# A hybrid decoder layer on one core: convolution taps handed out per attention unit, and two gate projections laid between the heads' q, k, v

## The chip, the cores and the metric

The kernel runs on 1 core of one Trainium2 chip. The metric is the device time of one execution in microseconds (us); lower is better. A run's time is given as the median of several executions; a profile is one execution more, with its own time. Engines are named as in the profile: PE is TensorE (matrix products), DVE is VectorE, ACT is ScalarE, POOL is GpSimd, SP issues most DMAs.

## The reference

One layer works on 512 prompt tokens and on 32 sample tokens (8 sequences of 4), with 1024 channels. Three branches read the same input and are merged by sigmoid gates; a feed-forward part follows.

```python
h = x @ w_in                                    # pooling input, q, k, v, conv input, 3 x 1024 gate columns
gates = jax.nn.sigmoid(h[..., o3:] + b_gate).reshape(B, T, N_BRANCH, D_MODEL)
p, new_pool = _pool_branch(u_a, pool_buf, start_pos)
br_a = jnp.einsum('btgc,gcd->btgd', p, pool_w).reshape(B, T, D_MODEL) * pool_scale
o = stick-breaking attention of 8 heads of 64 channels
br_b = o.reshape(B, T, W_ATT) @ w_att_o
glu = c_in[..., :W_CONV] * jax.nn.sigmoid(c_in[..., W_CONV:])
cc, new_conv = _dwconv(glu, conv_buf, conv_dw, conv_b)          # causal, 31 taps, 256 channels
br_c = jax.nn.silu(_layernorm(cc, conv_ln_g, conv_ln_b)) @ conv_pw
merged = gates[:, :, 0] * br_a + gates[:, :, 1] * br_b + gates[:, :, 2] * br_c
x = layernorm(ALPHA * x + merged @ w_out);  x = layernorm(ALPHA * x + ffn(x))
```

The sample tokens also attend to 1024 older keys and values each, which lie in pages of a cache.

## The kernel before

**Layout.** Channels lie on partitions and the 544 tokens on the free axis, cut into two halves of 288 (32 sample and 256 prompt tokens) and 256. Every operand of a large product is split into a high and a low part (`split_psum`, lines 210 to 216, and `_Weights.prepare`, lines 130 to 132), and `gemm` (line 218) issues three matmuls for each of 8 blocks of 128 input channels: 24 matmuls for 128 output channels of one half, 48 for both halves, 96 for a gate group of 256 channels.

**Weights.** `_Weights` holds a list of groups in the order of their use. SP loads each group, ACT makes the high part (line 131), DVE the low part (line 132), two chunks ahead.

**Stages.** First come the pooling input, the convolution input and its gate (lines 346 to 400). Then the pooling projection (lines 495 to 510): eight rounds, each with six matmuls (line 504) into the one PSUM pair "z", which ACT (line 510) and DVE (line 508) read. `gate0(g)` (line 489) makes 256 channels of the pooling branch's gate: 96 matmuls, which ACT evicts from PSUM (line 483), a sigmoid (line 486), and two products with the merged tile `mg` on DVE (line 492). Groups 0 and 1 come ahead of attention (`NGA`), group 2 behind the first scores, group 3 in the sample stage.

**Attention.** For each pair of heads `hp`, `qkv_q`, `qkv_k` and `qkv_v` project q, k and v. Their tiles are in the pool "att", opened after the pools "s1" and "pp" of the pooling branch are closed (lines 511, 512, 604). A unit is one pair of heads and one block of 128 queries; there are 16. `front` of the next unit (scores at line 574 into "z", then DVE and ACT up to line 585) comes ahead of `back` of this one (transposes at line 595, products at line 600). Behind units 0, 1 and 2 of a pair stands one of q, k and v of the next pair.

**Convolution.** `conv_work` (line 411) is a generator of 33 steps: two for the sample tokens, then 31 with one tap of each of two channel blocks, which are DVE instructions (lines 427 and 429). `pump(n)` takes n steps. `conv_norm` (line 436) transposes the result on PE, normalizes it and writes `ch` and `cl`, which the sample stage reads. The pool "cvp" of all this is closed behind the unit loop (line 624), and then "sam" is opened, which holds the sample stage's K and V (`kr`, `vr`).

**Order.** The program is written for `tile.TileContext(nc, schedule_with_timeline_sim=True)`: the compiler orders the instructions of each engine by a list schedule, in which the order of the text gives the priority. PSUM has three banks "mm" for products by `gemm`, one pair "z", two banks "tp" and one "o".

Of the kernel before, what the change touches and what calls it, by code (L numbers as in the profile page):

```python
# [50 lines left out]
NCST = 1160  # L51
E_ID, E_RC, E_IW, E_EPS = 0, 128, 158, 160
NEARLY = 161
NGA = 2
NGB = 3
PUMP = 4
NV1 = 31
GACT = 3
VACT = False
CNU = 0  # L60
KRB = 6
LNP = (True, False)
PSM = 5
# [31 lines left out]
class _Weights:  # L95
# [39 lines left out]
    def next(self):  # L135
        i = self.at
        self.at += 1
        for j in range(i, i + 1 + self.ahead):
            self.prepare(j)
        if i + self.ahead + 1 < len(self.chunks):  # L140
            for _ in self.load(self.chunks[i + self.ahead + 1][0]):
                pass
        return self.split.pop(i)
# [3 lines left out]
def hybrid_layer_kernel(  # L147
# [37 lines left out]
    gate_group = lambda br, g: w.group(win(GO + br * D + g * 256, 256), KD, 256, ((0, 128), (128, 128)))  # L185
    w.group(pool_w.rearrange("(c s) k d -> (s k) c d", s=2), 2, 256, ((0, 256),))
    for g in range(NGA):
        gate_group(0, g)
    for hp in range(4):
        for o in (256, 768, 1280):  # L190
            w.group(win(o + hp * P, P), KD, P, ((0, 128),))
        if hp == 0:
            for g in range(NGA, NGB):
                gate_group(0, g)
    steps = []
    for g in range(4):
        steps += [(2, g), (1, g), (3, g)]
# [90 lines left out]
    def exp_set(ins):  # L288
        with tc.issue_after(ins):
            nc.scalar.preload_act_table_set("natural_log_exp_and_others")  # L290
# [35 lines left out]
    def late_constants():  # L326
        nc.sync.dma_start(ct, cst)
        nc.sync.dma_start(pix, pidx)
        nc.sync.dma_start(piv, pidv)
        nc.sync.dma_start(rwc, rowc)  # L330
        nc.sync.dma_start(sbt, sbr)
        nc.vector.scalar_tensor_tensor(out=pix, in0=pix, scalar=128.0, in1=rwc[:, 0:1].to_broadcast([P, 8 * DB]), op0=ALU.mult, op1=ALU.add)
        nc.vector.scalar_tensor_tensor(out=piv, in0=piv, scalar=32.0, in1=rwc[:, 1:2].to_broadcast([P, 2 * DB]), op0=ALU.mult, op1=ALU.add)
# [137 lines left out]
    def pump(n):  # L471
        for _ in range(n):
            next(cw, None)
# [3 lines left out]
    def gates(br, g, pool_, tag, bufs=1, **kw):  # L477
        gt = pool_.tile([P, 2, T], F32, tag=tag, bufs=bufs, name=f"gt{br}{g}", **kw)
        for m in range(2):
            for (c0, c1), ps in zip(HALVES, chunk_psums(w.next(), X, KX)):  # L480
                bias = vcol(V_BG + br * 8 + 2 * g + m)
                if br == 0 and g < GACT:
                    nc.scalar.activation(gt[:, m, c0:c1], ps[:, :c1 - c0], AF.Identity, bias=bias)
                else:
                    nc.vector.tensor_scalar(gt[:, m, c0:c1], ps[:, :c1 - c0], bias, None, op0=ALU.add)
        return gt, nc.scalar.activation(gt, gt, AF.Sigmoid)


    def gate0(g):
        gt, ins = gates(0, g, mp_, "gt", GTB)  # L490
        for m in range(2):
            nc.vector.tensor_tensor(out=mg[:, 2 * g + m], in0=mg[:, 2 * g + m], in1=gt[:, m], op=ALU.mult)
        return ins
# [19 lines left out]
    late_constants()  # L513
    for g in range(NGA):
        ins = gate0(g)


    def qkv_q(ap, hp):
        qh = ap.tile([P, NP], F32R, tag="qh", name=f"qh{hp}")
        ql = ap.tile([P, NP], F32R, tag="ql", name=f"ql{hp}")  # L520
        for hf, ps in enumerate(chunk_psums(w.next(), X, KX)):
            a = hf * PH
            split_psum(qh[:, a:a + PH], ql[:, a:a + PH], prompt_of(ps, hf), 0.125)
            for s in range(2 if hf == 0 else 0):
                r = slice(64 * s, 64 * s + 64)
                h = 2 * hp + s
                nc.scalar.mul(qbd[r, hp, :, DS * h:DS * h + DS], sview(ps[r, :NS], DS), 0.125)
        return qh, ql

    def qkv_k(ap, hp):  # L530
        kh = ap.tile([P, NP], F32R, tag="kh", name=f"kh{hp}")
        kl = ap.tile([P, NP], F32R, tag="kl", name=f"kl{hp}")
        kf = ap.tile([P, T], F32, tag="kf", bufs=1, name=f"kf{hp}")
        for hf, ps in enumerate(chunk_psums(w.next(), X, KX)):
            a = hf * PH
            split_psum(kh[:, a:a + PH], kl[:, a:a + PH], prompt_of(ps, hf))
            c0, c1 = HALVES[hf]
            nc.scalar.copy(kf[:, c0:c1], ps[:, :c1 - c0])
        nc.gpsimd.tensor_copy(ksf[:, hp], kf[:, :NS])
        nc.gpsimd.dma_start(k_t[hp * P:(hp + 1) * P], kf)  # L540
        return kh, kl
# [62 lines left out]
    with pool("att", 2, reuse_waits="tile") as ap:  # L604
        exp_set(ins.ins)
        qq, kk, vv = {0: qkv_q(ap, 0)}, {0: qkv_k(ap, 0)}, {0: qkv_v(ap, 0)}
        units = [(hp, i) for hp in range(4) for i in range(4)]
        rcs = {0: front(ap, 0, 0, qq[0], kk[0])}
        for g in range(NGA, NGB):
            ins = gate0(g)  # L610
            exp_set(ins.ins)
        for u, (hp, i) in enumerate(units):
            if u + 1 < len(units):
                h1, i1 = units[u + 1]
                rcs[u + 1] = front(ap, h1, i1, qq[h1], kk[h1])
            back(ap, hp, i, rcs.pop(u), vv[hp])
            if hp < 3 and i < 3:
                fn, d = ((qkv_q, qq), (qkv_k, kk), (qkv_v, vv))[i]
                d[hp + 1] = fn(ap, hp + 1)
            pump(PUMP)  # L620
            if u == CNU:
                pump(100)
                exp_set(conv_norm().ins)
# [88 lines left out]
    for b in range(DB):  # L712
        g = b // 2
# [7 lines left out]
        for br, g in [c for c, n_ in zip(steps, at_batch) if n_ == b]:  # L721
            if br == 2:
                gt2, ins = gates(2, g, mp_, "gt", GTB)
# [10 lines left out]
            elif br == 1:  # L734
                gt, ins = gates(1, g, g1p, f"g1{g}")
# [215 lines left out]
    def down_out(ps, r, m, hf):  # L951
        n = HALVES[hf][1] - HALVES[hf][0]
        nc.vector.tensor_tensor(out=r, in0=ps[:, :n], in1=r, op=ALU.add)

        def put(ts, n_, tp):
            nc.scalar.copy(y2[:n_, ts, m * P:(m + 1) * P], tp)

        ins = to_tokens(r, hf, put)
        if m in STAT:
            norms[hf].stats(STAT.index(m), *STATC[STAT.index(m)])  # L960
        return ins
# [23 lines left out]
    for hf in range(2):  # L985
        with tc.high_priority():
            ins = down_out(fin[hf], rr[hf], m, hf)
# [21 lines left out]
        for k, v in enumerate((v0, v1)):  # L1009
# [6 lines left out]
            for c0, c1 in ((0, D),) if hf == 0 or k == 0 else ((0, 640), (640, D)):  # L1016
                ins = nc.vector.scalar_tensor_tensor(out=v[:, c0:c1], in0=v[:, c0:c1], scalar=rs[:, k:k + 1], in1=bq[:, c0:c1], op0=ALU.mult, op1=ALU.add)
# [74 lines left out]
```

## Time and profile before

| | |
|---|---|
| median of 3 runs | 883.52 us (881.38 to 885.2) |
| the profiled execution's own time | 882.96 us |
| its span, first to last instruction | 881.2 us |
| busy: PE, DVE, ACT, POOL | 96%, 54%, 39%, 15% of the span |
| PE on the chain that ended last | 87% of the span |

A row of a busy table gives, for each engine, the time in which it had work, and in brackets the number of instructions; PEld is PE's loading of weights. PEclk is the TensorE clock that was granted, as a share of full speed. In rows of a timeline stand the start in us, the time, engine and line, operation, out<-in, and in square brackets the idle time of the engine before it and what ended it. L226 is line 226 of the kernel. Matmuls overlap in the pipeline, so that the rows' times add up to more than the stretch that they take.

### The profile page before, as it was taken

What the parts mean: (1) busy time and instruction counts of PE and PEld (TensorE: products, weight loads), DVE (VectorE), ACT (ScalarE), POOL (GpSimd) and SP (SyncE); (2) the same over time, 40 slices, a digit from 0 to 9 for tenths busy, and PEclk for the clock granted to TensorE, in tenths of its full rate; (3) what the DMA queues carried; (4) which work ended last, traced back from release to release, by engine and by line L of the source; (5) the groups of instructions that cost most, each with busy time, mean ns of one, the idle gap of its engine ahead of it and who ended that gap; (6) DMA issues with size and microseconds to landing.
All of it is one profiled execution on the core that took longest, in us unless ns stands there. A gap on an engine that the chain in (4) does not pass through costs nothing.

```text
span 881.2 us, 16355 instructions
## 1 busy us (share of the span) xinstructions
PE 847.7 (96%) x6937; PEld 801.6 (91%) x6937; DVE 476.0 (54%) x853; ACT 344.7 (39%) x575; POOL 135.4 (15%) x158
## 2 busy tenths in 40 slices
PE   7998899999999999999999999999999999999993
PEld 6997899888897678789999999999999999999993
DVE  4899956888555444468656333333333333334437
ACT  5434377777653333344414323233332233222211
POOL 1430000002457686210001000000000000000002
PEclk9999799999999999999999999999999999999997
DMA  9413222413749889663600223332233323322322
GB/s 295 122 50 101 61 86 64 143 39 93 255 135 312 285 312 331 222 234 125 193 1 1 67 78 96 97 94 65 82 96 97 96 67 90 91 83 74 104 71 102
DMA packets 96393, 110.36 MB, mean 125 GB/s; under 512 B 4416, under 2 KB 88224, under 8 KB 94144
## 3 DMA queue, kind: packets, MB, share of 16 engines
q1 hardware_dynamic: 87840, 73.12, 27.0%
q0 software_dynamic: 8480, 36.20, 11.6%
q8 instruction: 54, 0.88, 0.4%
q14 instruction: 19, 0.16, 0.1%
HBM read 104.44 MB, written 4.87 MB: 124 GB/s over the span
## 4 chain that ended last, share of the span: by engine, by line
PE 87%; DVE 7%; DMA 2%; issue 2%; POOL 1%; ACT 1%; SPq 0%; DVEq 0%; ACTq 0%; POOLq 0%
PE mm L226 77%; DVE acc L429 3%; PE z L668 2%; PE o L694 1%; PE z L574 1%; PE o L600 1%; PE tp L595 1%; DVE wl L132 1%; DMA vr<-in_cv,piv 1%; POOL kr L637 1%; PE tp L811 1%; DMA kr<-in_ck,pix 1%; DMA raw<-in_w_in 1%; PE tp L877 1%; DVE y L1015 0%
## 5 line engine op out<-in xcount | busy, mean ns | idle before, releaser
L132 DVE TENSOR_TENSOR wl<-raw,wh 128x1024 fp32r<-128x1024 f32 (+1 forms) x129 | 151.8, 1180 | 139.1 <-ACT wh L131 138.2
L131 ACT CAST wh<-raw 128x1024 fp32r<-128x1024 f32 (+1 forms) x129 | 129.3, 1006 | 237.9 <-PE mm L226 213.2
L226 PE MATMUL mm<-xh,wh 128*128 128x256 f32 (+1 forms) x672 | 199.2, 297 | 7.6 <-ACT wh L131 5.8
L226 PE MATMUL mm<-x1l,wh 128*128 128x288 f32 (+1 forms) x704 | 202.7, 288 | 0.0
L226 PE MATMUL mm<-x1h,wl 128*128 128x288 f32 (+1 forms) x704 | 201.4, 287 | 0.0
L226 PE MATMUL mm<-x1h,wh 128*128 128x288 f32 (+1 forms) x704 | 200.5, 286 | 0.1
L226 PE MATMUL mm<-xl,wh 128*128 128x256 f32 (+1 forms) x672 | 197.4, 294 | 0.2 <-DVE xl L213 0.2
L226 PE MATMUL mm<-xh,wl 128*128 128x288 f32 (+1 forms) x672 | 197.5, 295 | 0.0
L226 PEld LDWEIGHTS mm<-xh,wh 128*128 128x128 f32 x672 | 129.0, 192 | 13.0 <-ACT wh L131 6.2
L226 PEld LDWEIGHTS mm<-x1l,wh 128*128 128x128 f32 x704 | 132.2, 188 | 0.2
L226 PEld LDWEIGHTS mm<-xl,wh 128*128 128x128 f32 x672 | 128.7, 192 | 3.9 <-issue 2.9
L226 PEld LDWEIGHTS mm<-x1h,wh 128*128 128x128 f32 x704 | 132.0, 188 | 0.4 <-ACT sg L921 0.3
L226 PEld LDWEIGHTS mm<-x1h,wl 128*128 128x128 f32 x704 | 132.0, 188 | 0.0
L226 PEld LDWEIGHTS mm<-xh,wl 128*128 128x128 f32 x672 | 128.6, 192 | 3.3 <-issue 2.6
L226 PE MATMUL mm<-gl,wh 128*128 128x256 f32 (+1 forms) x352 | 101.7, 289 | 0.0
L226 PE MATMUL mm<-gh,wh 128*128 128x256 f32 (+1 forms) x352 | 101.3, 288 | 0.0
L226 PE MATMUL mm<-gh,wl 128*128 128x256 f32 (+1 forms) x352 | 100.8, 286 | 0.0
L637 POOL DMA_INDIRECT kr<-in_ck,pix x64 | 69.5, 1086 | 35.8 <-issue 14.9
L924 DVE TENSOR_TENSOR sg<-mm,sg 128x288 f32<-128x288 f32 (+1 forms) x44 | 19.4, 440 | 92.1 <-PE mm L226 92.1
L226 PEld LDWEIGHTS mm<-gl,wh 128*128 128x128 f32 x352 | 66.1, 188 | 0.1
L226 PEld LDWEIGHTS mm<-gh,wh 128*128 128x128 f32 x352 | 66.2, 188 | 0.0
L226 PEld LDWEIGHTS mm<-gh,wl 128*128 128x128 f32 x352 | 66.1, 188 | 0.0
(217 smaller groups left out, 1151.7 us busy)
## 6 DMA issues: line engine op xcount, KB each, us to landing
raw<-in_w_in SPq DMA_DIRECT2D x14, 1024.0 KB, 5.9
raw<-in_w_g SPq DMA_DIRECT2D x11, 1024.0 KB, 5.3
raw<-in_w_u SPq DMA_DIRECT2D x11, 1024.0 KB, 5.3
raw<-in_w_d SPq DMA_DIRECT2D x16, 512.0 KB, 4.1
raw<-in_w_in SPq DMA_DIRECT2D x12, 512.0 KB, 4.0
raw<-in_w_out SPq DMA_DIRECT2D x4, 1024.0 KB, 6.6
raw<-in_w_d SPq DMA_DIRECT2D x8, 384.0 KB, 3.5
raw<-in_w_att_o SPq DMA_DIRECT2D x4, 512.0 KB, 3.7
```

Source lines behind the costliest of these rows:

```text
L131: self.nc.scalar.copy(hi[:, a:b], v[:, a:b])
L132: self.nc.vector.tensor_tensor(out=lo[:, a:b], in0=v[:, a:b], in1=hi[:, a:b].bitcast(F32), op=ALU.subtract)
L226: ins = nc.tensor.matmul(ps[:, :n], lw, rr, start=first and s == 0, stop=last and s == len(steps) - 1)
L429: nc.vector.scalar_tensor_tensor(out=o, in0=v, scalar=dw, in1=o, op0=ALU.mult, op1=ALU.add)
L574: nc.tensor.matmul(zps[s][:, :wd], a[r, qs], b[r, :wd], start=n_ == 0, stop=n_ == 2)
L595: nc.tensor.transpose(tp[:, kb], rc[:, s, kb * P:(kb + 1) * P], ident)
L600: nc.tensor.matmul(op_[64 * s:64 * s + 64, :P], vtok[:, kb, 64 * s:64 * s + 64], ats[s][:, kb], start=kb == 0, stop=kb == i)
L637: nc.gpsimd.indirect_dma_start(out=kr[:, u].rearrange("p h c -> p (h c)"), out_offset=None, in_=ck, in_offset=bass.IndirectOffsetOnAxis(ap ...
L668: nc.tensor.matmul(zp[32 * jj:32 * jj + 32, :256], qbd[:, hp, b], kvt[b, "k", jj][:, :, hp], start=hp == 0, stop=hp == 3)
L694: nc.tensor.matmul(op_[32 * c:32 * c + 32], at[:, j], kvt[b, "v", j // 4][:, j % 4], start=j >= 4, stop=False)
L811: ins = nc.tensor.transpose(tp[:n, k * P:(k + 1) * P], src[:, t0 - c0:t0 - c0 + n], ident)
L924: nc.vector.tensor_tensor(out=sg, in0=pu[:, :n], in1=sg, op=ALU.mult)
```

## The change

The first gate group alone stays ahead of attention (`NGA` is 1). Groups 1 and 2 come behind unit 3 and unit 7, which are the last units of the first and of the second pair of heads, and their weights are put in that order into the list. The convolution's steps are taken three behind each unit instead of all behind unit 0, and `conv_norm` stands behind unit 12 instead of unit 0. No instruction of the layer's arithmetic is added or left out.

```diff
-NGA = 2
+NGA = 1
 NGB = 3
-PUMP = 4
+PUMP = 3
...
-CNU = 0
+CNU = 12
...
     for hp in range(4):
         for o in (256, 768, 1280):
             w.group(win(o + hp * P, P), KD, P, ((0, 128),))
-        if hp == 0:
-            for g in range(NGA, NGB):
-                gate_group(0, g)
+        if 0 < hp < 1 + NGB - NGA:
+            gate_group(0, NGA + hp - 1)
...
         rcs = {0: front(ap, 0, 0, qq[0], kk[0])}
-        for g in range(NGA, NGB):
-            ins = gate0(g)
-            exp_set(ins.ins)
         for u, (hp, i) in enumerate(units):
...
             if hp < 3 and i < 3:
                 fn, d = ((qkv_q, qq), (qkv_k, kk), (qkv_v, vv))[i]
                 d[hp + 1] = fn(ap, hp + 1)
+            if i == 3 and hp < NGB - NGA:
+                exp_set(gate0(NGA + hp).ins)
             pump(PUMP)
             if u == CNU:
                 pump(100)
```

## Rows read from the trace of the kernel before

**Rows 1.** The page's table of engines: busy us (share of span), instructions.

```profile
PE 847.7 (96%) x6937; PEld 801.6 (91%) x6937; DVE 476.0 (54%) x853; ACT 344.7 (39%) x575; POOL 135.4 (15%) x158
```

**Rows 2.** Busy times by stretch: stretch, length, engines, PEclk, DMA share, GB/s.

```profile
44.00:84.00 40.00, 38.95 (x313) 36.98 (x312) 39.93 (x59) 15.84 (x24) 6.94 (x7) 1.00 0.24 70
84.00:104.00 20.00, 14.26 (x95) 13.31 (x94) 19.22 (x31) 5.77 (x14) 0.75 (x2) 0.74 0.22 67
104.00:236.00 132.00, 130.95 (x1076) 117.48 (x1075) 96.95 (x181) 98.95 (x189) 23.35 (x29) 1.00 0.35 113
236.00:384.00 148.00, 142.84 (x1319) 117.08 (x1320) 72.47 (x143) 58.06 (x67) 80.77 (x81) 0.99 0.72 248
```

**Rows 3.** Line 429, the taps: durations in ns, then busy time in two stretches.

```profile
L429 DVE SCALAR_TENSOR_TENSOR acc<-ge,vt,acc x60: 736/742/1169, 44.8 to 108.9; 128x512 f32<-128x512 f32 x60
...
44.00:70.60 26.60, 16.27 (x22) 1.00 0.16 47
70.60:91.50 20.90, 14.55 (x21) 0.91 0.33 100
```

**Rows 4.** PE's gemm matmuls (line 226) by stretch: length, busy (number), PEclk, DMA.

```profile
46.45:52.80 6.35, 6.35 (x49) 1.00 0.36 106
53.30:59.90 6.60, 6.60 (x51) 1.00 0.00 0
60.40:66.50 6.10, 6.04 (x47) 1.00 0.30 85
67.00:70.60 3.60, 3.05 (x21) 1.00 0.03 7
71.10:77.10 6.00, 5.29 (x41) 1.00 0.27 79
77.60:84.70 7.10, 7.09 (x55) 1.00 0.48 148
...
92.20:103.77 11.57, 11.56 (x72) 0.76 0.22 69
107.80:116.80 9.00, 9.00 (x73) 1.00 0.51 147
```

**Rows 5.** PE's timeline: pooling projections (first rows of rounds) and the first scores.

```profile
70.59 0.40 PE L504 MATMUL z<-ph,wh 64*128 64x288 f32 x2 [0.49 <-DVE mg L508]
...
84.70 0.40 PE L504 MATMUL z<-ph,wh 64*128 64x288 f32 x2
...
86.61 0.39 PE L504 MATMUL z<-ph,wh 64*128 64x256 f32 x2 [1.24 <-DVE mg L508]
...
91.54 0.48 PE L574 MATMUL z<-kh,qh 64*128 64x128 f32 x2 [4.31 <-DVE mg L508]
```

**Rows 6.** DVE's timeline between the last two evictions of the pooling projection.

```profile
86.47 2.73 DVE L429 SCALAR_TENSOR_TENSOR acc<-ge,vt,acc 128x512 f32<-128x512 f32 x4
89.12 1.22 DVE L132 TENSOR_TENSOR wl<-raw,wh 128x1024 fp32r<-128x1024 f32 x1
...
90.92 0.48 DVE L508 TENSOR_SCALAR mg<-z,vt 128x256 f32<-128x256 f32 x1
```

**Rows 7.** ACT's timeline: the first two evictions of q.

```profile
88.48 0.65 ACT L215 ACTIVATE qh<-mm 128x256 fp32r<-128x256 f32 x2
```

**Rows 8.** Line 486, the gates' sigmoid: its table loads, durations in ns.

```profile
L486 ACT ACT_TABLE_LOAD  x3: 1283/1283/1283, 118.5 to 240.7; - x3
```

**Rows 9.** The convolution's norm: first transposes, last split, first use of its result.

```profile
L450 PE MATMUL tp<-et,acc x10: 270/272/273, 124.2 to 131.6; 128*128 128x128 f32 x8, 128*32 128x128 f32 x2
...
L226 PE MATMUL mm<-cl,wh x8: 278/288/301, 239.7 to 242.3; 128*128 128x288 f32 x4, 128*128 128x256 f32 x4
L213 DVE TENSOR_TENSOR cl<-cf,ch x2: 718/721/724, 147.8 to 153.4; 128x544 fp32r<-128x544 f32 x2
```

**Rows 10.** Timelines of the sample stage: POOL's first V load, PE's longest wait.

```profile
226.25 0.95 POOL L644 DMA_INDIRECT vr<-in_cv,piv  x1 [0.30 <-issue]
...
287.70 2.48 PE L694 MATMUL o<-vr,sat 128*32 128x512 f32 x16 [2.98 <-DMA vr<-in_cv,piv]
```

## The prediction

> **What bounds the kernel now.** I first read the table of engines: PE is busy 847.7 of 881.2 us [rows 1], so a change can only win where PE stands, or lose by making it stand longer. Next the busy times by stage [rows 2]: of the four stretches from 44 to 384 us one stands out, 84 to 104 us, with PE busy 14.26 of 20 us at a granted clock of 0.74; in the others it is busy 96% or more. The same view names the engine behind it: from 44 to 84 us VectorE (DVE) is busy for 39.93 of 40 us. The instructions of the taps' line [rows 3] say with what: 60 taps of 0.74 us (about 0.66 us apart, since their ends overlap), the first at 44.8 us, the last at 108.9 us. In the text those taps stand behind attention unit 0, yet they run beside the pooling projection. So the compiler's list scheduler sends an instruction as soon as its inputs are there, and text order only decides between ready ones. That fact carries this forecast.
>
> Then I followed PE from one pooling projection (L504) to the next. They share one PSUM pair "z": the next one must wait until DVE (L508) and ScalarE (L510) have read the last. Between the eight of them PE runs 49, 51, 47, 21, 41 and 55 gemm matmuls [rows 4], then nothing between the seventh, the eighth and the first attention product (L574): these start at 84.70, 86.61 and 91.54 us, after idle times of 1.24 and 4.31 us that L508 ended [rows 5]. DVE's order shows why the second is long: between the seventh and eighth L508 stand four taps, a weight split and another tap [rows 6]. Why does PE have nothing else? The 264 matmuls are gates 0 and 1 (96 each), q (48) and the first half of k (24). q and k hold all three "mm" banks, and they are not emptied before 88.48 us [rows 7], after the last projection: the tiles qh and ql are in a pool opened in the space of the pool that holds the projection's inputs (an inference from the code). Gate banks are emptied by ScalarE into another pool and don't have this wait. So gates 0 and 1 are the only filler of the pooling chain.
>
> **The change part by part.** The sum is made against the profiled execution, 882.96 us (span 881.2 and 1.76 around it), 0.56 below the median of 883.52.
>
> *Gate 1 leaves the stretch ahead of attention.* Its 96 matmuls go behind unit 3. That leaves 264 - 96 = 168 matmuls of filler, which is 49 + 51 + 47 + 21: the filler of the first four gaps. The fifth projection starts at 70.59 us as now [rows 5]; from there to the attention product are four gaps without filler. Two such gaps are in the trace: 86.61 - 84.70 = 1.91 us and 91.54 - 86.61 = 4.93 us. I take their mean, 3.42, as both occur side by side under the same load of taps: 4 x 3.42 = 13.7 us instead of the 20.95 us from 70.59 to 91.54, so this stretch is 7.3 us shorter. The 96 matmuls are paid later: 73 take 9.00 us at full clock [rows 4], 0.123 each, so 11.8 us. Net +4.5 us. With all gaps at 1.91 it is 7.6 - 20.95 + 11.8 = -1.5; with all at 4.93 it is 19.7 - 20.95 + 11.8 = +10.6.
>
> *The taps get a later place.* Three steps (six taps) behind each unit, units 0 to 10, instead of all behind unit 0. They are ready at 44 us either way and DVE has no other use for the time, so I expect them to fill 44 us onward as now, at the pace seen: 22 by 70.6 us and 21 in the next 20.9 us [rows 3]. At 84.3 us about 36 are done and 24 are left, against 17 at 91.5 us now. The first units' DVE work (scores, scan, subtraction) stands behind those 24 taps, 16 us of DVE time, until about 115 us. Cover: q, k, v of the next heads (144 matmuls, 17.8 us) and the moved gate. Lower bound 0, upper bound one wait as of [rows 5], 5 us; I take +1, nearer to cover, since PE is not idle between 92.2 and 103.8 us with 17 taps about [rows 4].
>
> *Gate 2 and two tables.* Gate 2 goes from ahead of unit 0 to behind unit 7; it was in the attention stage and stays there: 0. Gate 1's sigmoid is now between exponentials: two table loads more on ScalarE, 2 x 1.28 = 2.6 us [rows 8]. ScalarE is busy 98.95 of 132 us there [rows 2], which hides them: 0, and +2.6 without that cover. Each gate's weight load (SP's queue), two weight splits and two products with mg (DVE) move with it, in the same number; DMA is busy 0.35 of that stage and DVE 96.95 of 132 us [rows 2]: 0, within the bounds of the taps. POOL's queue is not touched.
>
> *The slow clock.* After the long wait 72 matmuls take 11.57 us instead of 72 x 0.123 = 8.9: 2.7 us lost at a granted clock of 0.76 [rows 4]. Four gaps instead of two give it the same occasion: 0, between -2.7 and +2.7.
>
> *The norm behind unit 12.* Now its first transpose is at 124.2 us and its last split ends at about 153.4 + 0.7 [rows 9], some 30 us. Sixteen units take 132 us, 8.25 each, so unit 12 ends near 104 + 13 x 8.25 = 211 us and the norm near 241, just when it is first used, at 239.7 us [rows 9]; PE has gate matmuls meanwhile. The same instructions are issued: 0, upper bound 3 us (a PE wait as the one for V, next). No earlier than that does the convolution's space come free; that is a rival below.
>
> *Sample stage.* With gate 1 inside attention, as much gate work of the sample stage, now run early, moves back there, and may fill the one long PE wait, 2.98 us for V [rows 10]: between -3 and 0. I take 0, as a load that is late stays late.
>
> Sum: 4.5 + 1 = +5.5 us, so 882.96 + 5.5 = **888.5 us**; on the median it is 0.56%. A measurement of this kernel tells about 0.5%, 4.4 us, from no change. The forecast's own range is 885 to 892: gaps of 2.6 to 4.3 us, half-way from the mean to either row.
>
> **The rivals.**
>
> *Slower still: every gap is like the long one.* DVE's order ahead of the last L508 has five taps and a weight split [rows 6]; if the scheduler always keeps DVE's queue that full, each gap takes 4.93 us: 882.96 + 10.6 + 1 = 894.6. For it: DVE is never idle from 44 to 84 us. Against: the gap of 1.91 us. It decides if four or more taps stand ahead of each of the last four L508. Chance 0.08. The Trainium skill (TensorE: Matmul & The Clock Gate, on engine queue depths) gives VectorE a strict first-in-first-out queue of eight entries: by that a gap could hold up to eight of these taps, by estimate 8 x 0.66 + 1.0 = 6.3 us, and the sum would be +16 us; the longest gap without filler in the trace is 4.93 us, which is within that rule.
>
> *Faster: the taps really go where they are handed out.* If the scheduler takes them only near their unit, L508 has no taps ahead of it. The idle 1.24 + 4.31 us and the 2.7 us of slow clock go: 882.96 - 8.2 = 874.7. For it: DVE has 132 - 96.95 = 35 us free in the attention stage [rows 2]. Against: 62 taps need 41 us and 35 are free over all of it, and taps already run far ahead of their place in the text [rows 3]. It decides if no more than some ten taps run before the first L574. Chance 0.22.
>
> *No change: the gaps are short.* With taps in the queue but L508 reached after one of them, each gap is like the 1.91 us one, the front part is -1.5, and with a little cover in the sample stage the sum is -2 to +3: about 883.5. For it: the gap from the seventh to the eighth projection, under the same taps. Against: the gap right after it. Chance 0.30.
>
> *Slower by the convolution's space.* K and V buffers of the sample stage are in a pool opened after the convolution's is closed. If V's buffers are in that space, the first V load, at 226.25 us now [rows 10], waits for the norm's end near 241: 15 us, of which DMA can catch up some, as it is busy 0.72 of that stage [rows 2]; half gives +7.5 on top of 4.5 + 1: 896. Decides if the norm ends after 226 us. For it: one space, used in turn. Against: the order of buffers is not in the trace. Chance 0.08.
>
> *It does not do what it says*: taps in the old order are what I expect for the time of most of them; that is part of the forecast, not a case of its own.
>
> **How the numbers follow.** The forecast (888.5) has 0.32, the two slower rivals 0.08 each, the faster one 0.22, no change 0.30. The forecast's own range reaches below 887.9, so a fifth of its chance counts as no change: slower by over 0.5% is 0.26 + 0.16 = 0.42, within 0.5% is 0.06 + 0.27 = 0.33, and faster 0.22 with the lower edge of no change, 0.25. The 8-in-10 range goes from 875 (the faster rival) to 897 (the space rival) and leaves out what lies beyond these two. Both signs hold much of the chance; the likeliest case's own range, 885 to 892, stands above.
>
> **What would show it.** Right: the first L574 earlier than 91.5 us, near 84; three or four L504 in a row without gemm matmuls between them; over 30 taps before that L574; a PE idle sum over 8 us between 70 and 90 us; the norm's transposes after 200 us. Wrong: most taps after 100 us with PE unbroken (faster), or L504 with filler taken from the next heads' q and k (no change). First V load after 235 us would show the space rival.

## The result and the profile after

The changed kernel takes 893.27 us in the median of four runs (892.1 to 894.66), the kernel before 883.25 (881.38 to 885.2) beside it: ratio 1.0101, 95% interval 1.008 to 1.0122. It is slower by 10.0 us; the forecast was 888.5, the range 875 to 897. The profiled execution took 894.66 us, 892.9 of it the span.

The table of engines answers to [rows 1]: TensorE (PE) has the same 6937 matmuls and is busy 4.2 us longer, in a span 11.7 us longer.

```profile
PE 851.9 (95%) x6937; PEld 806.7 (90%) x6937; DVE 478.5 (54%) x853; ACT 348.4 (39%) x577; POOL 134.5 (15%) x158
```

The fixed stretches of [rows 2] would mix a stage that grew with one that only moved, so I cut both kernels at the same four events: the first pooling projection, the first attention scores, the end of the last attention product, and the first matmul of the output projection of attention. This is the view the rest of the study uses. A row has, as in [rows 2], the stretch, its length, busy time and number for PE, PEld, DVE, ACT and POOL, then the granted clock, the DMA share and GB/s. First the kernel before:

```profile
45.86:91.54 45.68, 39.08 (x313) 36.67 (x313) 45.64 (x66) 18.57 (x30) 5.88 (x6) 0.96 0.25 73
91.54:235.68 144.14, 143.22 (x1152) 129.38 (x1152) 108.36 (x199) 101.73 (x195) 24.10 (x31) 0.98 0.34 108
235.68:384.13 148.45, 142.97 (x1321) 117.21 (x1321) 72.82 (x143) 58.33 (x68) 80.90 (x81) 0.99 0.72 249
```

And the changed kernel, same events:

```profile
47.10:87.94 40.84, 27.62 (x219) 25.28 (x218) 40.80 (x60) 13.85 (x23) 5.91 (x6) 0.86 0.19 56
87.94:252.76 164.82, 159.07 (x1248) 143.50 (x1248) 114.20 (x205) 110.12 (x204) 20.11 (x27) 0.95 0.30 90
252.76:395.81 143.05, 141.38 (x1320) 118.14 (x1321) 74.02 (x143) 58.31 (x68) 84.75 (x86) 0.98 0.79 277
```

The count of matmuls shows gate 1 going from the first stage to the second (1152 to 1248, its 96). The first stage is 4.8 us shorter, the second 20.7 longer, the third 5.4 shorter, and the changed kernel entered the first one 1.2 us later: 1.2 - 4.8 + 20.7 - 5.4 = 11.7 us, the whole difference of the spans. Gate 1 is worth 11.8 us by the prediction's 0.123 us a matmul. So three entries need a cause: the pooling stage gave back only 4.8 of 11.8 us (a loss of 7.0), attention grew by 8.9 us beyond the gate, and the sample stage returned 5.4. The busy column says in what form. In attention PE stands idle 5.75 us, not 0.92, and its matmuls take 4.0 us more than those of the kernel before and the gate's 11.8 us together. In the stage behind it PE stands 1.67 us, not 5.48, and is busy 1.6 us less.

PE's timeline in the pooling stage answers to [rows 5] (start, duration, instruction, in brackets the idle time before it and what ended it; the first row of each projection):

```profile
71.85 0.40 PE L503 MATMUL z<-ph,wh 64*128 64x288 f32 x2 [0.51 <-DVE mg L507]
...
74.90 0.39 PE L503 MATMUL z<-ph,wh 64*128 64x256 f32 x2 [2.39 <-DVE mg L507]
...
78.60 0.61 PE L503 MATMUL z<-ph,wh 64*128 64x288 f32 x2 [3.08 <-DVE mg L507]
...
82.34 0.58 PE L503 MATMUL z<-ph,wh 64*128 64x256 f32 x2 [2.65 <-DVE mg L507]
...
87.94 0.47 PE L573 MATMUL z<-kh,qh 64*128 64x128 f32 x2 [4.59 <-DVE mg L507]
```

The gemm matmuls in the gaps, answering to [rows 4]: the first four gaps have their 49, 51, 47 and 21, the last four none.

```profile
47.40:54.00 6.60, 6.30 (x49) 6.16 (x49) 1.00 0.34 100
54.30:61.00 6.70, 6.45 (x51) 6.40 (x51) 1.00 0.18 53
61.40:67.60 6.20, 5.90 (x47) 5.87 (x47) 1.00 0.31 89
68.00:71.80 3.80, 3.05 (x21) 2.82 (x21) 1.00 0.02 5
71.80:87.90 16.10, 0.00 (x0) 0.00 (x0) 0.66 0.12 33
```

Four bare gaps of 3.05, 3.70, 3.74 and 5.60 us, 16.1 in all. VectorE's (DVE's) timeline says what each waits for, and answers to [rows 6]: an eviction of the pooling projection, L507, behind convolution taps. Two gaps have five taps ahead of the eviction, the last has five, a weight split (L132) and one tap more; the first (eviction at 74.34 us, not shown) has three taps and a product of gate 0.

```profile
78.08 0.47 DVE L507 TENSOR_SCALAR mg<-z,vt 128x256 f32<-128x256 f32 x1
78.47 3.39 DVE L428 SCALAR_TENSOR_TENSOR acc<-ge,vt,acc 128x512 f32<-128x512 f32 x5
81.78 0.51 DVE L507 TENSOR_SCALAR mg<-z,vt 128x288 f32<-128x288 f32 x1
82.21 3.39 DVE L428 SCALAR_TENSOR_TENSOR acc<-ge,vt,acc 128x512 f32<-128x512 f32 x5
85.52 1.21 DVE L132 TENSOR_TENSOR wl<-raw,wh 128x1024 fp32r<-128x1024 f32 x1
86.65 0.74 DVE L428 SCALAR_TENSOR_TENSOR acc<-ge,vt,acc 128x512 f32<-128x512 f32 x1
87.32 0.47 DVE L507 TENSOR_SCALAR mg<-z,vt 128x256 f32<-128x256 f32 x1
```

At the other end of attention the norm now stands. Its transposes start at 219.7 us and its last split at 243.5 (124.2 and 153.4 before, [rows 9]). PE's waits from 234 to 254 us, with the last matmul of a gate ahead of them and the next one behind them; the kernel before has only the last two of these waits (0.73 and 0.94 us):

```profile
235.55 0.29 PE L225 MATMUL mm<-xh,wl 128*128 128x288 f32 x1
...
237.92 0.55 PE L462 MATMUL tp<-et,cna 128*128 128x128 f32 x3 [0.59 <-ACT cf L463]
239.55 0.70 PE L594 MATMUL tp<-et,rc 128*128 128x128 f32 x4 [0.80 <-ACT cf L463]
242.04 0.91 PE L594 MATMUL tp<-et,rc 128*128 128x128 f32 x3 [1.79 <-ACT at L595]
246.47 1.11 PE L594 MATMUL tp<-et,rc 128*128 128x128 f32 x4 [1.64 <-ACT rc L584]
250.78 1.97 PE L599 MATMUL o<-at,vtok 128*64 128x128 f32 x16 [0.68 <-ACT at L595]
253.70 0.58 PE L225 MATMUL mm<-xh,wh 128*128 128x256 f32 x1 [0.94 <-DVE gt L484]
```

These transposes (L594) wait for ScalarE (ACT), which has the norm's activations among attention's last ones; two of the waits are for ACT's reading of a norm's product (`cf`), which lies in one of the two "tp" banks that attention's transposes use too. And PE has nothing to lay between: from 235.55 to 253.70 us no matmul of a gate runs. The last three products of a gate stay in the three "mm" banks until DVE reads them, behind the end of attention:

```profile
253.15 1.31 DVE L484 TENSOR_SCALAR gt<-mm,vt 128x288 f32<-128x288 f32 x3
```

The kernel before reads three such products at 236.07 us, also just behind its end of attention (235.68), but its last gate matmul is only 4.0 us ahead of that end, not 17.2. The granted clock falls with the idle time, at both ends of attention:

```profile
80.00:90.00 10.00, 2.88 (x14) 2.43 (x15) 10.00 (x17) 3.25 (x9) 0.02 (x1) 0.50 0.18 51
90.00:100.00 10.00, 10.00 (x70) 10.00 (x68) 10.00 (x16) 1.99 (x4) 0.74 (x2) 0.80 0.15 36
...
240.00:250.00 10.00, 6.57 (x36) 4.32 (x35) 5.50 (x7) 5.28 (x10) 7.87 (x8) 0.53 0.57 163
```

And GpSimd's (POOL's) timeline answers to [rows 10]: the first K load, at 210.5 us before, waits for the first of the norm's two splits (`cl`, 238.85 to 239.57 us), and the first V load, behind eight K loads in the same queue, comes at 250.37 us, not at 226.25.

```profile
239.62 1.05 POOL L635 DMA_INDIRECT kr<-in_ck,pix  x1 [28.73 <-DVE cl L212]
...
250.37 0.95 POOL L642 DMA_INDIRECT vr<-in_cv,piv  x1 [0.30 <-issue]
```

### The profile page after: what moved, and what is told of

It reads as the page before. It is cut to its first block, busy times and chain, and to the rows that moved or that the text cites. A ratio compares the mean times of both kernels' runs of the same rounds, so it can differ in the third digit from the quotient of the medians.

```text
span 892.9 us, 16359 instructions
## 1 busy us (share of the span) xinstructions
PE 851.9 (95%) x6937; PEld 806.7 (90%) x6937; DVE 478.5 (54%) x853; ACT 348.4 (39%) x577; POOL 134.5 (15%) x158
## 4 chain that ended last, share of the span: by engine, by line
PE 88%; DVE 7%; DMA 2%; issue 1%; ACT 1%; POOL 1%; SPq 0%; DVEq 0%; ACTq 0%; POOLq 0%
PE mm L225 78%; DVE acc L428 3%; PE z L666 1%; PE o L692 1%; PE o L599 1%; PE z L573 1%; PE tp L594 1%; PE tp L809 1%; DMA vr<-in_cv,piv 1%; DVE wl L132 1%; DMA raw<-in_w_in 1%; PE tp L875 1%; DVE y L1013 0%; DVE mg L507 0%; ACT wh L131 0%
## 5 line engine op out<-in xcount | busy, mean ns | idle before, releaser
L132 DVE TENSOR_TENSOR wl<-raw,wh 128x1024 fp32r<-128x1024 f32 (+1 forms) x129 | 153.2, 1190 | 138.0 <-ACT wh L131 137.2
L635 POOL DMA_INDIRECT kr<-in_ck,pix x64 | 67.2, 1050 | 58.2 <-DVE cl L212 28.7
```

Source lines behind the costliest of these rows:

```text
L132: self.nc.vector.tensor_tensor(out=lo[:, a:b], in0=v[:, a:b], in1=hi[:, a:b].bitcast(F32), op=ALU.subtract)
L635: nc.gpsimd.indirect_dma_start(out=kr[:, u].rearrange("p h c -> p (h c)"), out_offset=None, in_=ck, in_offset=bass.IndirectOffsetOnAxis(ap ...
```

## The experiments

Twelve runs in three sets, each set on one chip beside runs of the kernel before. The chips differ: the kernel before takes 894.25 us (first set), 884.29 (second) and 897.85 (third). So times are compared inside a set, by ratio to the kernel before, and stages by the three rows above. The ratio is not always that of the medians: in the third set the two differ by up to 2.5 us.

### First set: the two halves alone, the norm earlier, another space

**Gates alone.** The changed kernel with the taps and the norm as before:

```
-PUMP = 3
+PUMP = 4
-CNU = 12
+CNU = 0
```

> The changed kernel with the convolution back behind unit 0 (PUMP 4, CNU 0), gates 1 and 2 where the change puts them. Front theory (the lost time is four pooling gaps without filler, net +7 us): first L573 near 88 us, the first K load near 210 us, time near 890. Norm theory (the lost time comes from the norm behind unit 12, which makes attention's last units and the K loads late): time within 2 us of the kernel before, 883.

Measured: 899.79 us, ratio 1.0063 (1.004 to 1.0086), +5.5 us. The pooling stage is that of the changed kernel (40.82 us, first scores at 87.2). The first K load is at 213.1 us. The gates' move alone costs about what the prediction gave it, which lies nearer to the front theory than to the norm theory.

**Convolution alone.** The kernel before with `PUMP = 3` and `CNU = 12`.

> The kernel before with the convolution handed out as in the change (PUMP 3, CNU 12), gates 1 and 2 where they were. Front theory: first scores near 91.5 us as before, time within 2 us of 883. Norm theory: first K load near 240 us, PE idle sum of over 5 us between 230 and 260 us, time near 888 to 893.

Measured: 909.38 us, ratio 1.0169 (1.0144 to 1.0195), +15.1 us. The pooling stage is that of the kernel before (45.73 us, first scores at 92.9). That is more than either theory gave. Attention shows the same waits for ACT in its last units, and its first K load is at 231.7 us.

**Norm behind unit 4.** The changed kernel with `CNU = 4`: three steps per unit up to unit 4, the rest of the taps and the norm behind it.

> The changed kernel with the rest of the taps and the norm behind unit 4 (CNU 4), taps three steps a unit up to there. Front theory: as the changed kernel in front (four gaps, first scores near 88 us), time near 890 to 893. Norm theory: first K load back near 210 us, no PE idle sum at 230 to 260 us; time 883 to 886 if the norm is the whole loss, near 890 if both count.

Measured: 903.94 us, ratio 1.0109 (1.0086 to 1.0132), +9.7 us; first K load at 213.3 us.

**The projection's inputs elsewhere.** The prediction inferred that q's tiles lie in the space of the pooling projection's inputs, and that this keeps q and k from filling the bare gaps. The changed kernel with that pool on the other side of the memory:

```
-    pp = pps.enter_context(pool("pp", reuse_waits="tile"))
+    pp = pps.enter_context(pool("pp", side="right", reuse_waits="tile"))
```

> The changed kernel with the pooling projection's inputs (pool pp) on the other side of SBUF, so that q's tiles no longer lie in their space. Front theory with the wait for that space: q, k, v fill the gaps between the pooling projections, no two of them follow each other without gemm matmuls, PE idle between 70 and 90 us under 3 us, time 5 to 9 us under the changed kernel, 884 to 888. If the banks are held by something else: the four gaps stay, time near 893. Norm theory: the loss at 230 to 260 us stays in either case.

Measured: 911.78 us, ratio 1.0191 (1.0164 to 1.0217), some 17 us slower than the kernel before and beyond both theories. The changed kernel itself was not run in this set; its attention stage took about the same elsewhere, and what is longer here is the stage behind it (162.50 us, 143.05 in the changed kernel). The pooling stage is unchanged to 0.02 us (40.82), four gaps stay bare, and ScalarE still takes q's eviction right behind the last one of the pooling projection:

```profile
83.36 0.47 ACT L509 ACTIVATE mg<-z,vt 128x256 f32<-128x256 f32 x1
83.72 0.65 ACT L214 ACTIVATE qh<-mm 128x256 fp32r<-128x256 f32 x2
```

So moving this one pool doesn't open the gaps, and the inference isn't borne out. Whether the attention pool's place in the text or another shared space holds q back was not tried further.

Four attention stages of this set, from the first scores to the last product, in the order gates alone (norm behind unit 0), norm behind unit 4, own space (norm behind unit 12), convolution alone (norm behind unit 12, without the moved gate):

```profile
87.20:243.20 156.00, 155.20 (x1245) 140.57 (x1245) 114.18 (x205) 110.36 (x205) 25.67 (x31) 0.98 0.36 115
```
```profile
87.36:245.88 158.52, 156.47 (x1248) 142.90 (x1248) 113.75 (x205) 109.37 (x204) 23.88 (x31) 0.97 0.35 113
```
```profile
87.16:250.47 163.31, 157.74 (x1248) 142.18 (x1248) 113.93 (x205) 110.14 (x204) 19.28 (x26) 0.95 0.29 90
```
```profile
92.86:244.87 152.01, 146.36 (x1152) 130.99 (x1152) 109.04 (x199) 102.83 (x195) 19.71 (x27) 0.95 0.29 87
```

The first three have the same work (three matmuls of 1248 aside), but the later the norm, the longer the stage: 156.0, 158.5, 163.3 us; with 11.8 us for the gate, the fourth would be 163.8. PE's idle time in it is 0.8, 2.1, 5.6 and 5.7 us, and the clock goes from 0.98 to 0.95. A norm behind unit 12 costs attention some 7 us against one behind unit 0, by one trace of each on this chip. The time without gate matmuls ahead of the end of attention goes the same way: 0.1, 1.3, 16.4 and 15.9 us.

### Second set: both kernels again, ScalarE's evictions, norm behind unit 8

**The changed kernel as it is.**

> The changed kernel as it is, on the chip of this set, as the anchor for the runs beside it. Front theory (the pooling rounds run without matmuls of a gate between them) and norm theory (the norm stands in attention's tail and the first K load waits for its end) both expect what its first trace showed: ratio 1.010 (1.007 to 1.013), four bare gaps of about 4.0 us each, first attention scores at 87 to 88 us, first K load at 238 to 240, attention's last product near 252. If the set is taken on the chip with the slower sample stage, the ratio may reach 1.019.

Measured: 891.45 us, ratio 1.0083 (1.0062 to 1.0105), +7.2 us.

**The kernel before as it is.**

> The kernel before as it is, for a trace on the chip of this set: ratio 1.000 (0.998 to 1.002). First scores at 91.5 us, first K load at 210.5, attention's last product near 235. What the sample stage takes here (128 us from its first scores to its last product in the first trace) says which part of the changed kernel's loss is the chip's.

Measured: 883.72 us, ratio 0.9991 (0.998 to 1.0003). Its three stages, then those of the changed kernel:

```profile
46.60:92.30 45.70, 39.12 (x314) 36.71 (x314) 45.66 (x66) 18.58 (x30) 5.89 (x6) 0.97 0.24 73
92.30:235.38 143.08, 142.16 (x1152) 128.33 (x1152) 108.38 (x199) 101.83 (x195) 24.11 (x31) 0.99 0.34 109
235.38:386.36 150.98, 144.49 (x1322) 117.61 (x1322) 72.86 (x143) 58.33 (x68) 81.24 (x81) 0.98 0.70 244
```
```profile
45.29:86.14 40.85, 27.61 (x217) 25.27 (x217) 40.81 (x60) 13.85 (x23) 5.93 (x6) 0.85 0.19 56
86.14:249.60 163.46, 157.72 (x1248) 142.32 (x1248) 114.12 (x205) 110.23 (x204) 19.23 (x26) 0.95 0.29 90
249.60:392.79 143.19, 139.84 (x1322) 117.07 (x1321) 74.16 (x143) 58.33 (x68) 87.12 (x87) 1.00 0.79 278
```

The account of the first traces holds: the pooling stage loses 7.0 us (4.85 of the gate's 11.8 given back), attention grows by 8.6 beyond the gate, the stage behind it is 7.8 shorter. One part of that return can be read: the kernel before waits 3.45 us for V at 287.89 us (2.98 at 287.70 in [rows 10]), and its longest wait for K there is 1.9 us; in the changed kernel K and V waits behind attention are 1.7 and 0.8 us in all.

```profile
287.89 1.94 PE L694 MATMUL o<-vr,sat 128*32 128x512 f32 x8 [3.45 <-DMA vr<-in_cv,piv]
```

The other part is PE's busy time, with the clock: for the same 1322 matmuls PE is busy 144.49 us at a granted clock of 0.98 in the kernel before and 139.84 us at 1.00 in the changed one. Idle time (3.1 us less) and busy time (4.65 us less) make up the 7.8 us.

**Both evictions of a projection on ScalarE.** The changed kernel, L507 and L509:

```
-                    if s:
-                        nc.vector.tensor_scalar(mg[:, mo, c0:c1], pss[s][:, :c1 - c0], vcol(V_PS + mo), None, op0=ALU.mult)
-                    else:
-                        nc.scalar.mul(mg[:, mo, c0:c1], pss[s][:, :c1 - c0], vcol(V_PS + mo))
+                    nc.scalar.mul(mg[:, mo, c0:c1], pss[s][:, :c1 - c0], vcol(V_PS + mo))
```

> The changed kernel with both evictions of each pooling round on ScalarE, so that none stands behind five convolution taps on VectorE. Front theory: the four bare gaps shrink from 4.0 us to about 2 us (six matmuls of 1.4 us in all overlap nothing, then an eviction of 0.5 us, a second of 0.5 us, and the hand-over), so the first attention scores come at 78 to 82 us instead of 87.5, and the end 4 to 9 us earlier than the changed kernel beside it, less what attention then loses to taps that are not yet done (12 taps of 0.75 us = 9 us of VectorE). Rival (the gap is TensorE's own order or the wait for a bank, not VectorE's taps): gaps stay at 4 us, the time within 2 us of the changed kernel. Second rival (attention is paced by VectorE from its start, whenever it starts): gaps shrink, scores come early, and the end moves by less than 3 us.

Measured: 890.07 us, ratio 1.0064 (1.0047 to 1.0082), 1.4 us ahead of the changed kernel, with overlapping intervals. PE's timeline of the last two projections and the first scores:

```profile
71.56 0.40 PE L503 MATMUL z<-ph,wh 64*128 64x288 f32 x2
...
73.21 0.39 PE L503 MATMUL z<-ph,wh 64*128 64x256 f32 x2 [0.98 <-ACT mg L506]
...
76.40 0.33 PE L570 MATMUL z<-kh,qh 64*128 64x128 f32 x2 [2.57 <-ACT kh L211]
```

Only two bare gaps are left, 1.65 and 3.19 us, no wait there is for VectorE, and the first scores come at 76.4 us instead of 86.1. That settles what made the gaps long: the taps ahead of the evictions in VectorE's queue. But the 9.7 us don't reach the end. Of the gain at the first scores (9.7 us), 6.6 is left at the last attention product and 1.6 at the output projection: attention takes 166.64 us, 3.2 more than in the changed kernel (a wait of 1.99 us for q's first rows on ACT is the one new row), and the stage behind it 148.15, 5.0 more, with these waits:

```profile
PE z L663 <- DMA kr<-in_ck,pix: 3.3, 1, 3.3
PE o L689 <- DMA vr<-in_cv,piv: 1.0, 2, 0.8
```

By its number the second rival is right (less than 3 us), by its mechanism it isn't: most of the time is lost in the sample stage, not in attention on VectorE.

**Norm behind unit 8.** The changed kernel with `CNU = 8`.

> The changed kernel with the norm behind unit 8 instead of unit 12. Norm theory: the transposes of the norm move from 220 to about 185 us, the split ends before 215, the first K load goes back to about 213 us, TensorE's idle time between 236 and 262 us falls from 6.5 us to under 2 and its clock there stays up; the end comes 6 to 11 us earlier than the changed kernel beside it. Rival (the gates laid into attention cost the time, the sample stage is paced by TensorE or by its gathers whenever it starts): K loads early, but the end within 3 us of the changed kernel beside it. Third (the norm costs attention the same wherever it stands in it): last attention product still near 252 us.

Measured: 893.34 us, ratio 1.008 (1.0051 to 1.0108), no different from the changed kernel by the intervals. The executions are spread: two took 888.3 and 888.8 us, four 893.3 to 895.8, and the trace is of the slowest but one (895.5). The norm's transposes start at 186.8 us. Attention is 2.5 us shorter than in the changed kernel (160.92 us) and the stage behind it 5.0 longer (148.17). The K loads go only to 226.1 us, not to the expected 213: in POOL's queue they now stand behind v's output, which starts at 224.25 us, after 23.33 us in which POOL is idle until v is there:

```profile
224.25 0.76 POOL L552 DMA_DIRECT2D out<-vtok  x1 [23.33 <-DVE vtok L551]
...
226.07 1.05 POOL L635 DMA_INDIRECT kr<-in_ck,pix  x1 [0.31 <-issue]
```

The norm theory's 6 to 11 us are refuted on this chip: even the two fastest executions are 3 us ahead of the changed kernel. What is left is its rival: K loads 11 us earlier, the end the same. And a thing that no theory had: here the norm's last split ends at 217 us, 31 us ahead of the end of attention, yet PE starts no gate matmul in attention's last 14.0 us (16.3 in the changed kernel), and from 235 to 248.3 us it is busy 9.69 of 13.3 us at a granted clock of 0.68. So the norm's activations among the last units are not all of attention's loss.

### Third set: the halves again, ScalarE's evictions in the kernel before

**Gates alone, again.** The kernel of the first set.

> The gates moved as in the change, the taps and the norm as before (four taps per unit, norm behind unit 0). Ledger theory: the changed kernel loses 6 to 7 us of TensorE in the bare pooling gaps, about 8 us where the norm stands in attention's last units, and gets 5 to 8 us back in the sample stage, where TensorE then waits less for gathers. With the norm early neither the loss nor the return is there: ratio 1.005 to 1.008 (4 to 7 us), attention's last product at 242 to 243, first K load near 213. Rival (the taps per unit, not the gaps, cost the time): ratio under 1.003.

Measured: 907.84 us, ratio 1.0092 (1.0063 to 1.0122), +8.3 us (0.0092 x 897.85; by the medians +10.0). The ratio is above the expected range, the interval overlaps that of the first set; the taps-per-unit rival is out. Attention's last product, expected at 242 to 243 us, ends at 249.36: the attention stage is 161.22 us, 5.2 longer than the 156.00 of the first set. PE has 9.3 us of waits on gemm matmuls that nothing in the profile ends ("issue"), 15 of them, but only 3.2 us of these in attention and 6.1 behind it.

**Convolution alone, again.**

> The taps three per unit and the norm behind unit 12, the gates as before. Ledger theory, on a chip with the sample stage of the first traces: attention ends 8 to 9 us later than in the kernel before, the sample stage takes 6 to 8 us less, ratio 0.999 to 1.004. On the chip with the slower sample stage nothing is returned and the ratio is 1.015 to 1.019, as it was there. Rival (the late norm costs what it costs, wherever): ratio over 1.008 on either chip.

Measured: 906.57 us, ratio 1.0085 (1.0057 to 1.0112), +7.6 us (0.0085 x 897.85). Neither of the two figures of the ledger theory (gains and losses added up by stage): more than 1.004, less than 1.015. The rival's threshold, 1.008, is just met, but the interval reaches below it. Attention takes 151.76 us as in the first set (152.01), and in the stage behind it PE waits 8.8 us for two evictions of gates. The first, 5.03 us, is DVE's reading of the three products left in the banks; DVE came to it only at 249.06 us, 4.5 us behind the end of attention, after a wait for which the profile knows no instruction ("remote"):

```profile
248.71 0.41 DVE L656 COPY znf<-z 32x256 f32<-32x256 f32 x1 [7.19 <-remote]
```

The traced execution (910.28 us) is the slowest of seven, 3.7 us above their median.

**ScalarE's evictions with the gates alone.** The edit of the second set on the gates-alone kernel.

> As the gates-only kernel, with both evictions of each pooling round on ScalarE. Front theory: first attention scores at 76 to 78 us, 10 us before the gates-only kernel's, no norm in attention's tail; attention's last product at 232 to 235; the end 3 us earlier to 2 us later than the kernel before (ratio 0.996 to 1.002), 4 to 9 us ahead of the gates-only kernel. Rival (the sample stage is paced by its gathers on GpSimd, which issues 8 K loads in 10.4 us and V loads behind them, and takes back what comes early): less than 3 us ahead of the gates-only kernel, TensorE waits of 3 us and more for K or V near 285 us.

Measured: 898.44 us, ratio 1.0002 (0.9982 to 1.0021), 9.4 us ahead of gates alone by the medians. First scores at 76.7 us, end of the last attention product at 239.0, later than expected (232 to 235). Here nearly all of the front's 11.4 us arrives: the stage behind attention is 159.19 us, not longer than the 161.10 of gates alone.

**ScalarE's evictions in the kernel before.** The same edit there.

> The kernel before with both evictions of each pooling round on ScalarE: gate 1 still fills the rounds, but the long wait of 4.3 us ahead of the first scores and the one of 1.2 us shrink to about 2.5 and 0: first scores 2 to 4 us earlier (88 to 90), the end 0 to 4 us earlier, ratio 0.995 to 1.000. Rival as above (the sample stage takes it back): ratio 0.999 to 1.001.

Measured: 890.30 us, ratio 0.9888 (0.9849 to 0.9927): faster than the kernel before by 10 us (0.0112 x 897.85; by the medians 7.6), and more than either theory gave. Its pooling stage beside that of convolution alone in the same set, which is that of the kernel before:

```profile
45.10:90.34 45.24, 45.24 (x361) 42.82 (x360) 44.66 (x62) 24.09 (x43) 6.87 (x7) 1.00 0.25 74
```
```profile
47.13:92.82 45.69, 39.08 (x313) 36.68 (x313) 45.65 (x66) 18.60 (x30) 5.89 (x6) 0.97 0.24 73
```

Nearly the same length, but PE is never idle in it, at full clock, and has done 48 matmuls more, those of the second half of k and the first half of v: 48 x 0.123 = 5.9 us of work is out of attention (137.10 us), and the first scores stand 0.4 us earlier after the first projection. With gates 0 and 1 both there and every eviction free of the taps, filler lasts through all eight projections (the last one starts at 75.14 us). That is 6.4 of the 10 us; where the rest comes from would need a trace of the kernel before on this chip, which was not taken.

## Why the prediction was right or wrong

**The end.** Slower, as forecast, and inside the range; but the forecast's own sum was +5.5 us and the traces have +11.7, and 893.27 us lies above the forecast's own range of 885 to 892. That it lies under 897 is in part luck: the two terms that came out too small add up to 11.3 us more than forecast (2.4 for the gate, 8.9 for the norm), and 5.4 us that came back in the sample stage, put at nothing, hide half of it. (Spread evenly, two fifths of that own range lie below 887.9 us, not the fifth that the chances use.) The signs it needed are all there: first scores earlier than 91.5 us (87.94, forecast near 84), four projections in a row without gemm matmuls, 41 taps ahead of the first scores (forecast 36), 13.2 us of PE idle time at the rows of 71 to 88 us, the norm's transposes at 219.7. So is the sign of the space rival, the first V load after 235 us.

**Gate 1 leaves the stretch ahead of attention: right mechanism, size short.** Forecast +4.5, measured +6.9 (11.8 less 4.86, from the fifth projection to the scores). The mis-sized step is the mean gap, 3.42 us, taken as the mean of a short and a long one; the four are 4.02 on average. In these four gaps the order doesn't alternate: three to six taps stand ahead of every eviction. "Every gap is like the long one" had the right condition (four taps or more ahead of the evictions: in three of four) but the price of a gap with a weight split in it, 4.93; without one, five taps make 3.7. The gates-alone runs, +5.5 and +8.3 us, bear the term out end to end.

The Trainium skill (TensorE: Matmul & The Clock Gate, on engine queue depths) gives VectorE eight entries in strict order; it does not say how many instructions a program's order may put ahead of an eviction, so the prediction's 6.3 us per gap was its own estimate. The longest gap measured is 5.60 us, with seven instructions ahead of the eviction, which neither bears that estimate out nor refutes it.

**The taps get a later place: right that they don't.** 46.1 to 105.9 us, as before; on the first half of attention they cost no PE wait that the trace shows, so the +1 measured 0. The slow clock came out as forecast there too: with gates alone PE is busy 155.2 us in attention, and 143.2 before plus the gate's 11.8 is 155.0.

**The norm behind unit 12: the step that failed.** Forecast 0 with an upper bound of 3 us, as "PE has gate matmuls meanwhile" and "the same instructions are issued". In attention's last units PE has no such cover: the gate matmuls end at 235.55 us, 17.2 us ahead of the end of attention, as three products wait unread in the three "mm" banks. Its next work is the transposes of attention itself, which wait for ACT in the same queue as the norm's activations. Attention grew by 8.9 us beyond the gate (8.6 in the second set), and with the norm behind unit 0 instead of 12 some 7 us of it are not there (156.00 against 163.31 in the first set). The time of the norm's end was forecast well (241 us, measured 243.5 + 0.7), and that it is "just when first needed" too; its start (219.7, forecast 211) and its length (24.5 us, forecast 30) were off by errors that partly cancel. What was missed is who else needs ACT then, and that the gates' matmuls run out. How the 8.9 us divide between the two is not shown; with the norm out of the tail (behind unit 8) the second stays, and attention is only 2.5 us shorter.

**The sample stage: beyond the lower bound.** Forecast 0, at best -3; measured -5.4 and -7.8 in the two pairs of traces. The V wait of [rows 10] went (0.6 us of waits for V are left), as the lower bound had it; the rest is other waits and the clock, which the bound did not count.

**The space rival: happened, but wasn't the cost.** K loads wait for the convolution's space (28.73 us of POOL idle time, ended by the norm's first split), and V loads only stand behind them in POOL's queue; that V's own buffers wait for the space, as the rival had it, is not shown. Yet where K loads came 11 us earlier (norm behind unit 8) the end didn't move, and the stage behind attention is shorter with the late loads than in the kernel before, in both pairs of traces. The price put on it, +7.5 us, is not seen there.

**What stays open.** The norm's loss and the sample stage's return nearly cancel on the chip of the second set (norm behind 8 or 12: same time), but the convolution half alone costs 15.1 and 7.6 us on the other two chips, where the stage behind attention isn't shorter: 161.66 us against 157.27 with gates alone in the first set, 166.89 against 161.10 in the third. So the sum of the changed kernel is explained stage by stage, but not why the return comes on some chips only; the waits that nothing in the profile ends are seen on those two. There DVE too waits for releases that the profile knows no instruction for ("remote"): 30.3 and 30.5 us with the convolution half alone, 8.1 and 22.4 with gates alone, none in any trace of the first pair or the second set. What they are is not shown. Nor is it shown why q and k don't fill the bare gaps, or why the last three gate products are read only behind attention.

## What to carry to other kernels

An eviction that stands on the path of the busiest engine should not be on an engine whose queue is full of ready, unhurried work: five taps of 0.74 us in front of a 0.5 us eviction made two of the four bare gaps 3.7 us long, and putting both evictions on the engine with free time was worth 1.1% in the kernel before, where filler was there too, and no more than 1.4 us in the changed kernel. When filler is moved out of such a chain, count the queue ahead of each release, not the mean of two gaps. And work that is moved "behind" something is free only if the engines that it uses are not those that the last units there wait for, and if the work that should cover it does not run out before them.

## What the runs showed of the hardware

The same program differs between chips by as much as this change or more: the kernel before takes 884.29, 894.25 and 897.85 us in the three sets. Gates alone has an attention stage of 156.00 us on one and 161.22 on another; on the second 3.2 us of PE waits in it (9.3 with the stage behind) are ended by no event of the profile. A gain or loss of a few microseconds in the sample stage seen on one chip was not there on the next.

The granted clock falls behind idle time and rises again behind work. In the changed kernel it is granted at 0.50 in the ten microseconds with 2.88 us of PE work (half of 2.4 GHz, so the lower level throughout) and still at 0.80 in the next ten, when PE is busy without a break; where the evictions left no idle time (the last experiment) the whole stage stood at 1.00. Not all idle time lowered it: with both evictions on ScalarE the changed kernel's pooling stage has 3.6 us of idle time in 30.6 and stood at 1.00.
